# Moving the DRAM weight sums out of the half-size group, and two norm multiplications half a unit later, in a one-core hybrid decoder layer

## The chip, the cores and the metric

The kernel runs on one core of a Trainium2 chip. The metric is the device time of one execution in microseconds (us); lower is better. The core's engines are named as in the profile: PE (TensorE, matmuls), PEld (its weight loads), DVE (VectorE), ACT (ScalarE), POOL (GpSimd) and SP (SyncE). SP and POOL do no arithmetic here that matters; they issue DMA transfers, each from its own queue, in program order. Every engine takes its instructions in the order of its own list, so an instruction that waits holds up all that stand behind it on that engine.

## What is computed

One layer of a decoder for 512 positions and width 1024, in float32: a norm, one wide projection, two token mixers side by side (a block-sparse attention A and an mLSTM B), their gated sum, an output projection, and a SwiGLU feed-forward part, then a last norm. Cut to what matters here:

```python
u = rms_norm(x); z = u @ w_in            # q, k, v | mLSTM q, k, v, gates | branch gates ga, gb
hb = mlstm_chunkwise(q, k, v, i, f)      # (4 heads x 128)
hb = hb * rsqrt(mean(hb * hb) + eps)     # the heads' own norm
yb = sigmoid(ob) * hb * mlstm_norm_g
merged = sigmoid(ga) * (ya @ w_proj_a) + sigmoid(gb) * (yb @ w_proj_b)
h = x + merged @ w_out
u = rms_norm(h); g, up = split(u @ w_gate_up)
h = h + (silu(g) * up) @ w_down
return rms_norm(h)
```

## The kernel before, in words

**Products in three parts.** Each float32 matrix is split into a high and a low part (`split_hl`: ACT rounds the high part, DVE subtracts to get the low part), and a product is three matmuls: high by high, low by high, high by low. A weight block arrives by DMA as `raw` (128 x 1024, 512 KB), is split into `wh` (ACT) and `wl` (DVE), and is then multiplied on PE.

**Seven products instead of eight.** The projection for `gb` and the two large matrices of the feed-forward part are computed as 2 x 2 block products by a scheme with seven block products, named W11, S1, S2, W12, S3, S4, W22. The S blocks of the weights are sums of W blocks. Many of these sums are not made on an engine: a generator, `sum_steps`, makes them in DRAM, each by a copy (SP's queue, L854) into a scratch tensor `ws` and then an adding transfer onto it (POOL's queue, L857). There are 48 such steps: 8 for `gb` (called gs), then copies and additions for five pairs of feed-forward weights (gc0, ds0, gc1, ds1 and so on, S1 and S3 of each). A gc transfer is 1 MB, a ds transfer 512 KB. `make_sums(n)` issues steps until n have been issued; each step waits for the matmul that was last recorded in `st["mm"]` at that point, and this paces the transfers by PE's progress.

**Units.** The work up to the feed-forward part is a list of 66 units, each with one raw weight block: 0 to 13 are q, k, v and two output gates of the mixers, 14 to 17 `vb`, 18 to 25 `qkb`, 26 and 27 `ob`, 28 to 35 `ga`, 36 to 49 `gs` (the half-size group: seven products of two units each, 12 matmuls in a unit and not 24), 50 to 57 `p` (the two branch projections of one column block), 58 to 65 `wo`. `fill` runs the next unit: it first splits the weights of units ahead (two ahead, three within the gs group: before unit 44 runs, unit 47 is split), then calls `make_sums`, then runs the unit's matmuls. Attention and mLSTM steps are woven between the units. `PE` meets all of them in one fixed order.

**Loads.** Raw blocks lie in nine buffers; a load is issued on SP's queue when the split of an older block has freed its buffer. Copies for the sums stand in the same queue between the loads.

**The heads' norm.** After the last mLSTM head, `ml_norm` (L1864 on) takes the root on DVE and ACT, stores the four rows to DRAM (`nd`, POOL, L1873) and reads them back spread over all partitions (`nb`, POOL, L1876, one transfer for heads 0 and 1 and one for heads 2 and 3). `ml_e(h)` then multiplies: L1890 by `nb`, L1891 by the norm weight and the sigmoid of `ob`, both on DVE, then a split into `yb` (ACT and DVE). Heads 2 and 3 also have to be issued after the evacuation of S3 (L663). The order at the end of the mixers is: one unit, `ml_norm`, four gs units (40 to 43), `ml_e(0)`, `ml_e(1)`, two gs units (44, 45), `ml_e(2)`, `ml_e(3)`, the remaining gs units (46 to 49), then the p units, which need `yb` in the second half of each.

**Feed-forward part.** Items gc0, gc1, ds0, gc2, ds1, gc3, ds2, gc4, ds3, then a remainder. A gc item is seven products of 5.44 us, a ds item seven of 2.72 us. In `gc_run` one more sum step is issued with some of the products. Its loads have due times of their own (`GLD`, `plan`), so that a block's load does not move when a sum step moves.

A planner orders the instructions of each engine by priority (in the manner of a list, with its own model of when an operand is ready), so the order on an engine follows the program's order closely but not exactly.

Of the kernel before, what the change touches and what calls it, by code (L numbers as in the profile page):

```python
# [76 lines left out]
G0 = UNITS.index(("gs", 0))  # L77
# [22 lines left out]
def hybrid_layer_kernel(ctx: ExitStack, tc, xT, wall, wgb, wgc, wgu, wds, wdl, g3v, vecs, wgates, consts, rope, out):  # L100
    nc = tc.nc
    V, A, T = nc.vector, nc.scalar, nc.tensor
# [11 lines left out]
    def nm(p="t"):  # L114
        cnt[0] += 1
        return f"{p}{cnt[0]}"

    def slot(dt=F32, name="a"):
        return act.tile([P, S], dt, name=nm(name), tag="A")
# [11 lines left out]
    def mmb():  # L131
        return psum.tile([P, S], F32, name=nm("mm"), tag="mm", bufs=3)
# [120 lines left out]
    for k in range(KT):  # L253
        for j in (0, 2) if k == 0 else (0,):
            c = slice(j * P, (j + 2) * P if k == 0 else S)
# [27 lines left out]
    uh, ul = [], []  # L283
# [23 lines left out]
    for k in range(KT):  # L307
        if k < 4:
            t = blk2(F32R, "u", raw=k < 2)
            h, l = t[:, 0, :], t[:, 1, :]  # L310
        else:
            h, l = slot(F32R, "uh"), slot(F32R, "ul")
        wh, wl = w0h[k // 4][:, k % 4], w0l[k // 4][:, k % 4]
        halves = [(0, 1), (2, 3)] if k == 0 else [range(4)]
        c = slice(0, P * len(halves[0]))
# [12 lines left out]
        for js in halves:  # L328
            if js[0]:
                c = slice(2 * P, S)  # L330
# [67 lines left out]
    def fill(n=1, mid=None):  # L398

        for _ in range(n):  # L400
            u = pos[0]
            if u >= len(UNITS):
                if mid:
                    mid()
                return
            kind, i = UNITS[u]
            ahead = min(u + LOOK + 1, max(u, G0 + 2 * len(GW))) if kind == "gs" else u + LOOK
            while wstate["split"] <= min(ahead, NGEN - 1):
                split_unit()
            pos[0] += 1  # L410
            v = u if u < G0 else max(u + G0, 2 * u - 2 * len(GW)) // 2
            make_sums(5 * (min(v, G0 + 4) - 19) // 4 + 3 * max(v - G0 - 10, 0) // 4)
            g = run[kind](i, *whl.pop(u))
            next(g, None)
            if mid:
                mid()
            for _ in g:
                pass
# [10 lines left out]
    st = {"made": 0}  # L429
# [49 lines left out]
    def run_v(kind):  # L479
        def products(ps, t, units):  # L480
            c = slice(t * P, (t + 1) * P)
            for j, (wh, wl) in units:
                for e in range(2):
                    k = 2 * j + e
                    h, l = wh[:, S * e : S * e + S], wl[:, S * e : S * e + S]
                    T.matmul(ps, uh[k][:, c], h, start=k == 0, stop=False)
                    T.matmul(ps, uh[k][:, c], l, start=False, stop=False)
                    T.matmul(ps, ul[k][:, c], h, start=False, stop=k == KT - 1)

        def evacuate(ps, t):  # L490
            c = slice(t * P, (t + 1) * P)
            for j in range(2):
                d = st[kind, j]
                o = ps[:, 256 * j : 256 * j + 256]
                if kind == "va":

                    o = o.rearrange("p (h d) -> p h d", h=4)
                    h, l = d[:, :, t * P : t * P + 64], d[:, :, t * P + 64 : (t + 1) * P]
                else:
                    o = o.rearrange("p (h d) -> p h d", h=2)  # L500
                    h, l = d[:, 0:4:2, c], d[:, 1:4:2, c]
                act_(h, o, AF.Copy, scale=rt[:, t : t + 1])
                V.scalar_tensor_tensor(l, o, rt[:, t : t + 1], f(h), op0=ALU.mult, op1=ALU.subtract)

        def fn(i, wh, wl):
            if i == 0:
                st[kind] = []
                st[kind, "ps"] = [mmb(), mmb()]
                for j in range(2):
                    d = st[kind, j] = slot4(F32R, kind)  # L510
                    if kind == "vb":
                        vml[2 * j], vml[2 * j + 1] = (d[:, 0, :], d[:, 1, :]), (d[:, 2, :], d[:, 3, :])
                    for e in range(4 if kind == "va" else 0):
                        vat[4 * j + e] = d[:, e, :]
            st[kind].append((i, (wh, wl)))
            for t in range(2):
                products(st[kind, "ps"][t], t, st[kind][-1:])
            yield
            if i == 3:
                for t in range(2):  # L520
                    evacuate(st[kind, "ps"][t], t)
                for t in range(2, 4):
                    ps = accb() if kind == "va" else mmb()
                    products(ps, t, st[kind])
                    evacuate(ps, t)
        return fn
# [370 lines left out]
    def make_sums(n):  # L897

        while st["made"] < n:
            st["made"] += 1  # L900
            i = next(making, None)
            if i is not None:
                tc.add_manual_dep(raw_ins(i), raw_ins(st["mm"]).name, after, reason="paced")
# [96 lines left out]
    def gc_run(c):  # L1000

        key = ("gc", c)
        g = sw.pop(key)
        two = range(2)

        def product(ps, w, o, first=False):
            make_sums(st["made"] + (w in (("S4", "W22"), ("W11", "S2", "S3", "W22"))[c > 0]))
            for j, (wh, wl) in enumerate(g[w]):
                for t in two:
                    at(key, w, 2720 * j + 1360 * t)  # L1010
                    q = slice(t * P, (t + 1) * P)
                    for e in range(2):
                        k = 2 * j + e
                        bh, bl = (b[:, q] for b in bop(o, k))
                        d = slice(e * S, (e + 1) * S)
                        st["mm"] = T.matmul(ps[t], bh, wh[:, d], start=first and k == 0, stop=False, skip_group_check=not first)  # L1016
                        T.matmul(ps[t], bh, wl[:, d], start=False, stop=False, skip_group_check=not first)  # L1017
                        T.matmul(ps[t], bl, wh[:, d], start=False, stop=k == 3, skip_group_check=not first)  # L1018

        def done(w, t):  # L1020
            at(key, w, 4080 + 1360 * t)

        def copies(ps, w, name):
            r = []
            for t in two:
                done(w, t)
                r.append(slot(name=name))
                act_(r[t], ps[t], AF.Copy)
            return r

        X = [mmb() for _ in two]
        product(X, "W11", 0, first=True)
        a = copies(X, "W11", "ga")
        Z = [sb() for _ in two]
        product(Z, "S1", 1, first=True)
        x3 = copies(Z, "S1", "gx")
        product(X, "S2", 4)
        b = copies(X, "S2", "gb")
        yield
        if c == 0:  # L1040
            second_norm(key)
        rg = st["rg"]
        Y = [accb() for _ in two]
        product(Y, "W12", 2, first=True)
        for t in two:
            done("W12", t)
            V.tensor_tensor(a[t], Y[t], a[t], op=ALU.subtract)
        yield
        product(X, "S3", 5)
        for t in two:  # L1050
            done("S3", t)
            V.tensor_tensor(x3[t], X[t], x3[t], op=ALU.add)
            act_(x3[t], x3[t], AF.Silu, scale=rg[:, t + 2 : t + 3])
        yield
        ht = slot4(name="ht").rearrange("p j (b h e x) -> p (j b) h e x", h=2, e=32, x=2)

        def turn(t, u, s):
            V.tensor_tensor(u, u, s, op=ALU.mult)
            V.transpose(ht[:, :, t // 2, :, t % 2], u.rearrange("p (b e) -> p b e", e=32))

        product(Z, "S4", 3)
        for t in two:
            done("S4", t)
            V.tensor_tensor(b[t], Z[t], b[t], op=ALU.add)
            at(key, "W22", 1360 * t)
            turn(t + 2, b[t], x3[t])
        product(X, "W22", 6)
        for t in two:
            done("W22", t)
            s = slot(name="gs")  # L1070
            act_(s, X[t], AF.Silu, scale=rg[:, t : t + 1])
            turn(t, a[t], s)
        at(key, "W22", 5440 + 3000)
        d = hid_t[c] = dram.tile([P, 4, S], F32, name=nm("ad"))
        for i in range(4):
            nc.sync.dma_start(
                d[:, i].rearrange("(g o) x -> o g x", o=32), ht[32 * i : 32 * i + 32].rearrange("p (g b) h e x -> p g (b h e x)", g=4)
            )
# [835 lines left out]
    while n < len(steps) or qa or qb:  # L1914
        if qa and (len(qa) >= LA or n >= len(steps)):
            kind, h, b, r = qa.pop(0)
            qb.append((kind, h, b, moba_b(h, b, r) if kind == "a" else r, n))
        if n < len(steps):
            kind, h, b = steps[n]
# [9 lines left out]
        def mid():  # L1929
            for g in todo.pop(n, ()):  # L1930
                add(g)
            advance(2 if n < 13 else 3)
            second()
# [9 lines left out]
        while qb and (qb[0][4] <= n - LC):  # L1943
            kind, h, b, r, _ = qb.pop(0)
# [14 lines left out]
        drain()  # L1959
    fill(1)  # L1960
    ml_norm()
    fill(4)
    ml_e(0)
    ml_e(1)
    fill(2)
    ml_e(2)
    ml_e(3)
    while pos[0] < len(UNITS) and UNITS[pos[0]][0] != "p":
# [102 lines left out]
```

## Time and profile before

| what | value |
|---|---|
| time, median of 3 runs | 716.77 us (715.41 to 717.86) |
| the profiled execution's own time | 716.61 us |
| its span, first to last instruction | 714.8 us |
| PE busy | 701.3 us, 98% of the span |
| DVE busy | 609.6 us, 85% |
| ACT busy | 460.9 us, 64% |
| moved by DMA | 170.79 MB, mean 239 GB/s |
| mean granted PE clock | 0.993 |

How to read it: PE's busy time is close to the span, so time is lost only where PE waits or where its clock is lowered, and at the two ends. The views used below are the page, tables of windows (busy time of each engine in a stretch, then the granted clock, then the busy share of the 16 DMA engines, then GB/s), lists of waits (total us, times, longest), and timelines of single engines (start, duration, engine, line, operation, tiles, count, and in brackets the idle time before it with what ended it). Times are us from the start of the span.

### The profile page before, as it was taken

Reading aid. Unit: us, or ns where it says so; the run is one execution under the profiler, and the core shown is the slowest. Engines: PE = TensorE matmul, PEld = TensorE weight load, DVE = VectorE, ACT = ScalarE, POOL = GpSimd, SP = SyncE. Lnnn points to the kernel's source line nnn. Section 1 sums busy time; section 2 is a strip of 40 time slices with the busy share of each in tenths; the row PEclk is TensorE's granted clock in tenths of the full one; section 3 lists DMA queues with packets and bytes.
Section 4 is the critical chain, followed back from the end, with each engine's and each line's share of the span. In section 5 each row is a group of like instructions: output and inputs, shape, how many; then the busy total and the mean of one; then the engine's idle time right before and its main releaser. Section 6 shows DMA issues by size and latency. Waiting matters only on the chain.

```text
span 714.8 us, 9624 instructions
## 1 busy us (share of the span) xinstructions
PE 701.3 (98%) x3248; PEld 582.6 (82%) x3248; DVE 609.6 (85%) x1009; ACT 460.9 (64%) x788; POOL 83.2 (12%) x118
## 2 busy tenths in 40 slices
PE   9999999999999999799999999999999999999995
PEld 6888888887888888688888888888888888888884
DVE  6888977898996866978699888898899899797996
ACT  6634888769784786567354756566765666575665
POOL 0013010000130001020010110012003004003000
PEclk9999999999999999899999999999999999999999
DMA  9769684479899899699987578889899959969703
GB/s 326 290 198 242 202 228 147 162 229 297 207 296 332 240 251 277 253 283 335 297 217 185 198 218 240 315 229 300 295 268 279 264 155 221 314 157 271 221 1 117
DMA packets 54881, 170.79 MB, mean 239 GB/s; under 512 B 6472, under 2 KB 10960, under 8 KB 49328
## 3 DMA queue, kind: packets, MB, share of 16 engines
q1 hardware_dynamic: 42544, 126.76, 51.2%
q0 software_dynamic: 12000, 42.87, 28.3%
q10 hardware_dynamic: 288, 0.56, 0.2%
q8 instruction: 25, 0.41, 0.2%
q14 instruction: 24, 0.20, 0.1%
HBM read 145.99 MB, written 64.01 MB: 294 GB/s over the span
## 4 chain that ended last, share of the span: by engine, by line
PE 77%; DVE 14%; ACT 4%; issue 2%; DMA 1%; DVEq 0%; ACTq 0%
PE mm L231 7%; PE mm L227 7%; PE mm L230 7%; PE mm L1017 5%; PE mm L1018 5%; PE mm L1016 5%; PE s L1017 3%; PE s L1018 3%; PE s L1016 3%; PE mm L1262 2%; PE mm L1264 2%; PE mm L1261 2%; PE mm L334 2%; PE acc L334 2%; DMA ws<-in_wgc_dram 1%
## 5 line engine op out<-in xcount | busy, mean ns | idle before, releaser
L163 ACT ACTIVATE w<-raw 128x1024 fp32r<-128x1024 f32 (+2 forms) x107 | 108.1, 1023 | 48.7 <-PE mm L1017 18.7
L991 DVE TENSOR_TENSOR w<-raw,w 128x1024 fp32r<-128x1024 f32 x70 | 84.4, 1220 | 19.8 <-ACT w L163 19.5
L176 DVE TENSOR_TENSOR wl<-raw,wh 128x1024 fp32r<-128x1024 f32 x62 | 75.2, 1221 | 16.2 <-ACT wh L163 16.1
L163 ACT ACTIVATE wh<-raw 128x1024 fp32r<-128x1024 f32 x62 | 65.1, 1054 | 31.1 <-PE mm L230 27.7
L1016 PE MATMUL mm<-w,bq 128*128 128x512 f32 x160 | 62.2, 389 | 0.0
L1017 PE MATMUL mm<-w,bq 128*128 128x512 f32 x160 | 62.2, 389 | 0.0
L1018 PE MATMUL mm<-w,bq 128*128 128x512 f32 x160 | 62.2, 389 | 0.0
L227 PE MATMUL mm<-u,wh 128*128 128x512 f32 x96 | 37.8, 394 | 0.0
L231 PE MATMUL mm<-u,wh 128*128 128x512 f32 x96 | 37.5, 391 | 0.0
L230 PE MATMUL mm<-u,wl 128*128 128x512 f32 x96 | 37.5, 390 | 0.0
L231 PE MATMUL mm<-ul,wh 128*128 128x512 f32 x96 | 37.4, 389 | 0.0
L227 PE MATMUL mm<-uh,wh 128*128 128x512 f32 x96 | 37.4, 389 | 0.0
L230 PE MATMUL mm<-uh,wl 128*128 128x512 f32 x96 | 37.3, 389 | 0.0
L1016 PEld LDWEIGHTS mm<-w,bq 128*128 128x128 f32 x160 | 30.0, 188 | 6.3
L1017 PEld LDWEIGHTS mm<-w,bq 128*128 128x128 f32 x160 | 30.0, 188 | 6.2
L1018 PEld LDWEIGHTS mm<-w,bq 128*128 128x128 f32 x160 | 30.0, 188 | 6.2
L1172 DVE TENSOR_TENSOR w<-raw,w 128x1024 fp32r<-128x1024 f32 x25 | 30.3, 1218 | 1.3 <-ACT w L163 1.2
L1261 PE MATMUL mm<-w,ac 128*128 128x512 f32 x80 | 31.2, 389 | 0.0
L1262 PE MATMUL mm<-w,ac 128*128 128x512 f32 x80 | 31.2, 389 | 0.0
L1016 PE MATMUL s<-w,bq 128*128 128x512 f32 x80 | 31.1, 389 | 0.0
L1017 PE MATMUL s<-w,bq 128*128 128x512 f32 x80 | 31.1, 389 | 0.0
L1018 PE MATMUL s<-w,bq 128*128 128x512 f32 x80 | 31.1, 389 | 0.0
(495 smaller groups left out, 2019.3 us busy)
## 6 DMA issues: line engine op xcount, KB each, us to landing
raw<-in_wall_dram SPq DMA_DIRECT2D x48, 512.0 KB, 6.0
raw<-ws SPq DMA_DIRECT2D x38, 512.0 KB, 6.9
raw<-in_wgc_dram SPq DMA_DIRECT2D x30, 512.0 KB, 7.5
ws<-in_wgc_dram SPq DMA_DIRECT2D x10, 1024.0 KB, 8.1
ws<-in_wgc_dram POOLq DMA_DIRECT2D x10, 1024.0 KB, 11.0
raw<-in_wds_dram SPq DMA_DIRECT2D x15, 512.0 KB, 7.6
ws<-in_wds_dram SPq DMA_DIRECT2D x10, 512.0 KB, 6.3
ws<-in_wds_dram POOLq DMA_DIRECT2D x10, 512.0 KB, 7.7
```

Of the source, the lines that this page charges most:

```text
L163: return A.activation(out_, in_, func, **kw)
L176: last["v"] = V.tensor_tensor(l, src, f(h), op=ALU.subtract)
L227: st["mm"] = T.matmul(ps, wh[:, c], rh[j], start=start and j == 0, stop=False)
L230: T.matmul(ps, wl[:, c], rh[j], start=False, stop=False)
L231: T.matmul(ps, wh[:, c], rl[j], start=False, stop=stop and j == n - 1)
L991: V.tensor_tensor(l, t, f(h), op=ALU.subtract)
L1016: st["mm"] = T.matmul(ps[t], bh, wh[:, d], start=first and k == 0, stop=False, skip_group_check=not first)
L1017: T.matmul(ps[t], bh, wl[:, d], start=False, stop=False, skip_group_check=not first)
L1018: T.matmul(ps[t], bl, wh[:, d], start=False, stop=k == 3, skip_group_check=not first)
L1172: V.tensor_tensor(w[k][1], g[k], f(w[k][0]), op=ALU.subtract)
L1261: T.matmul(ps, bh, wh[:, d], start=first and k == 0, stop=False, skip_group_check=not first)
L1262: T.matmul(ps, bl, wh[:, d], start=False, stop=False, skip_group_check=not first)
```

## The change

```diff
@@ fill
             v = u if u < G0 else max(u + G0, 2 * u - 2 * len(GW)) // 2
-            make_sums(5 * (min(v, G0 + 4) - 19) // 4 + 3 * max(v - G0 - 10, 0) // 4)
+            make_sums(5 * (min(v, G0) - 17) // 4 + 3 * max(v - G0 - 10, 0) // 4)
@@ run_v, products
-                    T.matmul(ps, uh[k][:, c], h, start=k == 0, stop=False)
+                    i = T.matmul(ps, uh[k][:, c], h, start=k == 0, stop=False)
+                    if kind == "vb":
+                        st["mm"] = i
@@ gc_run, product
-            make_sums(st["made"] + (w in (("S4", "W22"), ("W11", "S2", "S3", "W22"))[c > 0]))
+            make_sums(st["made"] + (w in (("S4", "W22"), ("W11", "S1", "S2", "S3", "W22"), ("W11", "S2", "S3", "W22"))[min(c, 2)]))
@@ the end of the mixers
     fill(1)
     ml_norm()
-    fill(4)
+    fill(5)
     ml_e(0)
     ml_e(1)
-    fill(2)
+    fill(1)
     ml_e(2)
     ml_e(3)
```

`G0` is 36, the first gs unit. The formula in `fill`, worked out for every unit, gives:

| units | sum steps issued before | sum steps issued after |
|---|---|---|
| 18 to 35 | 1 to 20 (the first at unit 20) | 1 to 22 (the first at unit 18) |
| 36 to 49 (gs) | 21 to 26, at units 36, 38, 40, 42 (two), 44 | 23, at unit 36 |
| 50 to 65 (p, wo) | 27 to 35, from unit 55 on | 24 to 32, from unit 55 on |
| gc0, gc1, gc2, gc3, gc4 | 2, 4, 4, 3, 0 | 2, 5, 4, 4, 1 |

Up to unit 36 every step comes two units sooner. Step 24 is the copy for gc2's S1, 25 the addition for ds1's S3, 26 the copy for gc2's S3. The three steps that the gs group no longer issues are caught up in the feed-forward part, in gc1, gc3 and gc4. The change in `run_v` adds no instruction: it records the `vb` units' matmuls, so that the step now issued at unit 18 waits for unit 17. The last part puts gs unit 44, with the split of unit 47 that goes ahead of it, in front of `ml_e(0)` and `ml_e(1)`; `ml_e(2)` and `ml_e(3)` keep their place after unit 45. No arithmetic is added or removed.

## The prediction

> **What bounds the kernel now.** I read the page's busy times first, then the waits of PE, then PE, DVE and POOL in order of time around the longest wait.
>
> ```profile
> PE 701.3 (98%) x3248; PEld 582.6 (82%) x3248; DVE 609.6 (85%) x1009; ACT 460.9 (64%) x788; POOL 83.2 (12%) x118
> PE s L639 <- DVE wl L176: 3.5, 1, 3.5
> PE s L250 <- DVE mask L238: 1.0, 1, 1.0
> ```
>
> PE is busy for 98% of the span, so there is little to win anywhere but in PE's waits. Only one is longer than 1 us: a matmul of the gs group that waits for the low part of a weight block.
>
> ```profile
> 283.50 0.39 PE L638 MATMUL s<-wh,uh 128*128 128x512 f32 x1
> ...
> 286.22 0.39 PE L638 MATMUL s<-wh,uh 128*128 128x512 f32 x1
> 290.15 0.79 PE L639 MATMUL s<-wl,uh 128*128 128x512 f32 x1 [3.54 <-DVE wl L176]
> ...
> 301.06 0.39 PE L227 MATMUL mm<-ya,wh 128*128 128x512 f32 x1
> 292.00:294.00 2.00, 2.00 (x6) 1.59 (x5) 2.00 (x4) 0.00 (x0) 0.00 (x0) 0.50 0.51 170
> ```
>
> A gs unit of 12 matmuls takes 286.22 - 283.50 = 2.72 us, 0.227 for each matmul. At 286.22 unit 47 (second half of S4) begins, and units 47, 48 and 49 should be through at 286.22 + 3 x 2.72 = 294.38, when the first p unit could begin. It begins at 301.06. **The place costs 6.68 us**, not 3.54: after the wait the granted clock is 0.50 (last row, third number from its end), and some 12 matmuls run at half speed.
>
> ```profile
> 279.48 1.30 DVE L666 STREAM_TRANSPOSE gt<-gW 128x512 f32<-128x512 f32 x2
> 286.34 1.29 DVE L1890 SCALAR_TENSOR_TENSOR nsb<-nb,nsb 128x512 f32<-128x512 f32 x2 [5.57 <-DMA nb<-nd]
> ...
> 288.88 1.22 DVE L176 TENSOR_TENSOR wl<-raw,wh 128x1024 fp32r<-128x1024 f32 x1
> 290.01 1.29 DVE L176 TENSOR_TENSOR yb<-nsb,yb 128x512 fp32r<-128x512 f32 x2
> 291.21 1.22 DVE L176 TENSOR_TENSOR wl<-raw,wh 128x1024 fp32r<-128x1024 f32 x1
> 292.35 1.41 DVE L663 SCALAR_TENSOR_TENSOR gS<-mm,nrt,gS 128x512 f32<-128x512 f32 x2
> ...
> 294.89 1.25 DVE L1890 SCALAR_TENSOR_TENSOR nsb<-nb,nsb 128x512 f32<-128x512 f32 x2
> ...
> 297.38 1.22 DVE L176 TENSOR_TENSOR wl<-raw,wh 128x1024 fp32r<-128x1024 f32 x1
> ```
>
> DVE stood idle for 5.57 us ahead of the first norm multiplication, waiting for `nb`. The split of unit 47 (288.88) is queued behind the four multiplications of heads 0 and 1, though its operands had long been there. So PE waits for a DMA that it does not need yet. From 286.34 on DVE has no gap: splits 47 and 48, two `yb` splits, S3's evacuation, four more multiplications, split 49.
>
> ```profile
> 272.31 0.60 POOL L1873 DMA_DIRECT2D nd<-fl  x1 [4.33 <-DVE fl L357]
> 272.90 0.86 POOL L857 DMA_DIRECT2D ws<-in_wds_dram  x1
> 277.73 1.13 POOL L1876 DMA_DIRECT2D nb<-nd  x2 [3.97 <-DMA nd<-fl]
> DMA to landing us min/median/max: 8.6/10.0/11.4
> 277.80 10.37 DMA ws<-in_wgc_dram
> ```
>
> Why `nb` is late: the 8 KB store `nd` is issued at 272.31, an addition for the sums (step 25) goes right behind it, `nb` can be issued only at 277.73, and its first transfer lands 8.6 us later. The last row is from the chain that ended last: it names the copy of step 26, which landed at 288.17, as what released a multiplication. That instruction reads no `ws` and DVE had no gap there, so I go by the wait on `nb`. Both transfers lie in the same stretch, and the change touches both.
>
> **The change part by part.**
>
> *No sums in the gs group.* Steps 22 to 26 leave it (3.5 MB, of them step 25 on POOL between `nd` and `nb`, and copies 24 and 26 on SP). What `nb` then costs isn't in the trace, so it is bounded.
>
> ```profile
> 414.01 0.52 POOL L1136 DMA_DIRECT2D row<-vec  x1 [7.70 <-DVE vec L357]
> 416.83 0.74 POOL L1137 DMA_DIRECT2D rg<-row  x1 [2.31 <-DMA row<-vec]
> h1d<-ht POOLq DMA_DIRECT2D x4, 256.0 KB, 4.8
> R<-scr POOLq DMA_DIRECT2D x4, 640.0 KB, 9.3
> ```
>
> The nearest store-then-load on POOL took 416.83 - 414.01 = 2.82 us, against 5.42 here, so `nb` is issued at about 272.31 + 2.82 = 275.1 (at worst 277.7). For its landing the rows on the same queue go from 4.8 us (256 KB) to 9.3 (640 KB, spread over the partitions like `nb`); I take the middle, 7.05, and get T = 282.2 for the time when `nb` is there. Bounds: 275.1 + 4.8 = 279.9 and, nothing gained, 286.34.
>
> *Norm multiplications one gs unit later.* Split 47 now stands ahead of `ml_e(0)`. DVE is free at 279.48 + 1.30 = 280.78; split 47 takes 290.01 - 288.88 = 1.13 and ends at 281.9, well ahead of unit 47's second matmul at 286.45. So the old wait goes. What is late next is **split 49**, still behind all eight multiplications. It ended 297.38 + 1.22 - 286.34 = 12.26 us after the first of them, 11.13 without split 47. Unit 49 would begin at 286.22 + 2 x 2.72 = 291.66, and its second matmul needs split 49 at 291.89. With T = 282.2 the split ends at 282.2 + 11.13 = 293.3: PE waits r = 1.4 us. By the bounds of T: r = 281.9 + 11.13 - 291.89 = 1.15 if `nb` is there by 281.9, and 5.6 if it still lands at 286.34. Split 48 (291.21 + 1.14 - 286.34 - 1.13 = 4.9 after T) ends at 287.1, ahead of its need at 289.2.
>
> Whether a wait of 1.4 us also costs clock lies between two rows.
>
> ```profile
> 173.64 0.55 PE L1735 MATMUL s<-con,P 128*128 128x128 f32 x3 [0.61 <-ACT P L168]
> 170.00:180.00 10.00, 9.39 (x50) 7.68 (x49) 9.94 (x28) 8.97 (x20) 0.00 (x0) 1.00 0.75 254
> ```
>
> After 0.61 us of idle PE the clock stayed at 1.00; after 3.54 it was 0.50, which cost 6.68 - 3.54 = 3.1 us, less 0.4 for a short second wait. I take no drop, since 1.4 is nearer to 0.61; the other end, 2.7 us more, is kept. The Trainium skill (TensorE: Matmul & The Clock Gate, "Part 1: The HAM clock gate") puts the drop to half rate after an idle window of about 3.4 us, free-running: by that rule a wait of 1.4 us costs no clock, and by the upper bound 711.3 below would become 714.0.
>
> *First sums two units sooner.* Copies and additions of steps 1 to 20 move ahead, past splits, loads and the reads of `R` in the SP and POOL queues. On POOL the tight one is the read of `R` for head 3.
>
> ```profile
> 196.47 0.58 POOL L1767 DMA_DIRECT2D R<-scr  x1 [9.53 <-PE s L1800]
> 204.66 0.35 DVE L1779 SCALAR_TENSOR_TENSOR R<-con,cS,R 128x128 f32<-128x128 f32 x1 [0.26 <-DMA R<-scr]
> 208.22 1.22 DVE L176 TENSOR_TENSOR wl<-raw,wh 128x1024 fp32r<-128x1024 f32 x1
> 219.05 0.40 PE L227 MATMUL mm<-u,wh 128*128 128x512 f32 x1
> ws<-in_wgc_dram POOLq DMA_DIRECT2D x10, 1024.0 KB, 11.0
> 263.52 3.22 SPq L207 DMA_DIRECT2D raw<-in_wgb_dram  x2
> ```
>
> DVE waits for `R` already now, 0.26 us. After the change an addition of 1 MB (11.0 us to landing) goes out shortly ahead of it, so DVE may idle up to 11 us. Cover: the split at 208.22 is for unit 31, whose matmuls begin at 219.05, 9.6 us after the split's end. I cost it at 0, with 11.0 - 9.6 = 1.4 at most; nothing can be gained, as PE has no wait there. SP's loads are far ahead (last row: units 48 and 49 were loaded from 263.5 on, 25 us ahead of their matmuls), so copies among them cost nothing. Recording `vb`'s matmuls adds no instruction.
>
> *Three sums later.* The p and wo units issue nine steps as before, 7 MB as before. The feed-forward part gets 1 MB more in gc1, 1 MB more in gc3 and 0.5 in gc4. I cost that at 0 because loads there are early.
>
> ```profile
> 426.00:464.00 38.00, 38.00 (x169) 31.50 (x168) 33.11 (x39) 22.25 (x30) 1.58 (x2) 1.00 0.88 277
> 483.00:521.00 38.00, 38.00 (x170) 31.46 (x169) 33.96 (x39) 24.87 (x33) 5.12 (x6) 1.00 0.97 288
> 480.01 7.61 SPq L912 DMA_DIRECT2D raw<-in_wgc_dram  x2
> raw<-in_wgc_dram SPq DMA_DIRECT2D x30, 512.0 KB, 7.5
> 514.10 1.07 ACT L163 ACTIVATE w<-raw 128x1024 fp32r<-128x1024 f32 x1
> q0 software_dynamic: 12000, 42.87, 28.3%
> ```
>
> In gc2 (483 to 521) the DMA engines are at 0.97 and PE is still busy for 38.00 of 38.00. The second load of W22 is issued by 480.01 + 7.61 = 487.6 and split at 514.10, 26.5 us later, of which the landing takes some 7.5.
>
> **The sum.** 716.61 (the profiled execution: span 714.8 and 1.8 around it) - 6.68 + 1.4 = **711.3 us**. The median of the runs shown, 716.77, is 0.16 above that execution, within the runs' own scatter (715.41 to 717.86), so I leave it out.
>
> **The rivals.**
>
> *Nothing left.* The planner puts split 49 ahead of heads 2 and 3, or `nb` is early and PE's order gives way: 716.61 - 6.68 = 709.9. For it: DVE idles until `nb` lands, so there is room; against it: in the order before, split 49 stood behind all eight. Chance 0.14.
>
> *The multiplications stay ahead of split 47.* The planner may keep its order; then only the earlier `nb` counts: split 49 ends at 282.2 + 12.26 = 294.5, r = 2.6, 712.5. Against it: the program's order is changed there, and it was followed before. Chance 0.09.
>
> *`nb` isn't sooner.*
>
> ```profile
> 280.00:290.00 10.00, 6.61 (x30) 5.14 (x28) 4.43 (x7) 1.67 (x3) 0.00 (x0) 0.94 0.98 375
> ```
>
> If loads of p units fill the freed DMA time, T stays 286.34 and r = 5.6, split into 2.1 ahead of unit 48 and 3.5 ahead of unit 49: 715.5, or 718.2 if the second one drops the clock again. For it: the DMA engines were at 0.98 in that stretch (last number but one); against it: the loads are paced by DVE's splits, one 512 KB block in 2.72 us. Chance 0.15, mostly the lower value.
>
> *The sums that were moved cost PE time later (slower).* The additions' queue took 28.3% of 714.8 us for 42.87 MB, 4.7 us of all engines per MB. In 426 to 464 (gc1) 12% of 38 us are free, 4.6 us, and 4.7 are added; in gc2 next to nothing is free. If loads then come late, gc1 and gc3 cost up to 4.7 us each: 711.3 + 9.4 = 720.7. It decides once a load lands 26.5 - 7.5 = 19 us later than now. The Trainium skill (DMA: Bandwidth & Descriptors, "Issuing engines are not separate DMA queues") speaks for it: transfers from any engine share the same 16 DMA engines, so moving steps in a queue saves none of their time. Against it stands gc2's full PE at 0.97. With a planner's order that is worse elsewhere, chance 0.12.
>
> **How the numbers follow.** The forecast has 0.50, and with the first two rivals **faster by over 0.3%** (below 714.6, about what a measurement can tell from no change) has 0.73; within 0.3% has the third rival's 0.15; slower has 0.12. The range goes from 709.4 (nothing left, less half a us of scatter) to 716.5, which takes in the third rival without the clock's drop and leaves out some 0.18.
>
> **What would show it.** Split 47 ahead of L1890 on DVE, no wait of PE at unit 47, POOL with nothing between `nd` and `nb`, `nb` issued near 275 and there by about 282, a short wait ahead of unit 49, and a clock of 1.00 through the group. From the first p unit to the end the distance should stay as before. It is wrong if PE waits in 388 to 654, or if `nb` still lands after 285.

## The result, and the profile after

| what | before | after |
|---|---|---|
| time, median | 715.66 us (715.41 to 717.86, 6 runs) | 711.17 us (710.59 to 711.74, 6 runs) |
| the profiled execution's own time | 716.61 us | 711.12 us |
| its span | 714.8 us | 709.3 us |
| mean granted PE clock | 0.993 | 0.997 |

The ratio of the times over all runs is 0.9931, with a 95% interval from 0.9917 to 0.9945 (the two medians alone give 0.9937): the kernel became faster by 0.7%. The page's busy times hardly show it, since PE's share stays at 98%:

```profile
PE 698.6 (98%) x3248; PEld 580.7 (82%) x3248; DVE 609.1 (86%) x1009; ACT 459.9 (65%) x788; POOL 83.1 (12%) x118
```

To find where the time went, mark the same matmuls in both traces: the first of unit 35, of the first p unit and of gc0. The timeline of PE before has two of them here (the third, 301.06, is in the prediction):

```profile
246.88 0.40 PE L227 MATMUL mm<-u,wh 128*128 128x512 f32 x1
...
388.39 0.39 PE L1016 MATMUL mm<-w,bq 128*128 128x512 f32 x1
```

and the timeline of PE after has, beside these three, the one matmul in the stretch that waits:

```profile
246.97 0.40 PE L227 MATMUL mm<-u,wh 128*128 128x512 f32 x1
...
293.06 0.50 PE L641 MATMUL mm<-wl,u 128*128 128x512 f32 x1 [0.69 <-DVE wl L176]
...
295.46 0.39 PE L227 MATMUL mm<-ya,wh 128*128 128x512 f32 x1
...
382.79 0.39 PE L1018 MATMUL mm<-w,bq 128*128 128x512 f32 x1
```

| stretch | before | after |
|---|---|---|
| start to unit 35 | 246.88 | 246.97 |
| unit 35 to the first p unit | 54.18 | 48.49 |
| first p unit to gc0 | 87.33 | 87.33 |
| gc0 to the end of the span | 326.41 | 326.51 |

All of the gain, 5.69 us, lies between unit 35 and the first p unit; elsewhere nothing differs by more than 0.1 us. The middle two distances are used for every run below. Next the cause, on POOL's timeline after:

```profile
272.41 0.61 POOL L1875 DMA_DIRECT2D nd<-fl  x1 [19.18 <-DVE fl L357]
275.22 1.11 POOL L1878 DMA_DIRECT2D nb<-nd  x2 [2.19 <-DMA nd<-fl]
```

Nothing stands between `nd` and `nb`, and they are 2.81 us apart instead of 5.42. The list of DMA issues in 262 to 290 (KB each, median us from issue to landing) had, before,

```profile
raw<-in_wall_dram SPq DMA_DIRECT2D x4, 512.0 KB, 11.6
...
nb<-nd POOLq DMA_DIRECT2D x2, 512.0 KB, 10.0
nd<-fl POOLq DMA_DIRECT2D x1, 8.0 KB, 5.1
```

and has after

```profile
raw<-in_wall_dram SPq DMA_DIRECT2D x6, 512.0 KB, 3.6
...
nb<-nd POOLq DMA_DIRECT2D x2, 512.0 KB, 5.7
nd<-fl POOLq DMA_DIRECT2D x1, 8.0 KB, 2.5
```

These three land in 31% to 57% of the time they took, the plain weight loads too: the stretch as a whole is less loaded. DVE's timeline after shows what became of its stall:

```profile
280.79 1.18 DVE L176 TENSOR_TENSOR wl<-raw,wh 128x1024 fp32r<-128x1024 f32 x1
281.90 1.28 DVE L1892 SCALAR_TENSOR_TENSOR nsb<-nb,nsb 128x512 f32<-128x512 f32 x2
...
284.42 1.22 DVE L176 TENSOR_TENSOR wl<-raw,wh 128x1024 fp32r<-128x1024 f32 x1
...
291.79 1.22 DVE L176 TENSOR_TENSOR wl<-raw,wh 128x1024 fp32r<-128x1024 f32 x1
292.93 1.29 DVE L176 TENSOR_TENSOR yb<-nsb,yb 128x512 fp32r<-128x512 f32 x2
```

The first row is split 47, then the first norm multiplication follows with no bracket, so without idle time: `nb` was there. Splits 48 and 49 follow at 284.42 and 291.79; split 49 is the one that is late, by 0.69 us. The waits of PE after (total us, times, longest) no longer hold anything over 1 us:

```profile
PE s L250 <- DVE mask L238: 1.0, 1, 1.0
PE s L1737 <- ACT P L168: 0.9, 2, 0.6
PE mm L641 <- DVE wl L176: 0.7, 1, 0.7
```

The tables of windows after (length, PE busy, PEld, DVE, ACT, POOL, clock, DMA share, GB/s) show the clock at 1.00 around the old wait, and PE without any gap in the feed-forward part, which got 2.5 MB more of sums:

```profile
286.00:295.00 9.00, 8.31 (x37) 6.55 (x36) 9.00 (x14) 3.52 (x5) 0.00 (x0) 1.00 0.48 166
...
388.00:654.00 266.00, 266.00 (x1188) 220.48 (x1187) 234.50 (x275) 168.54 (x224) 41.58 (x50) 1.00 0.89 259
```

### The profile page after: what moved, and what is told of

Its sections match the earlier page's. It is cut to its first block, busy times and chain, and to the rows that moved or that the text cites. A ratio compares the mean times of both kernels' runs of the same rounds, so it can differ in the third digit from the quotient of the medians.

```text
span 709.3 us, 9628 instructions
## 1 busy us (share of the span) xinstructions
PE 698.6 (98%) x3248; PEld 580.7 (82%) x3248; DVE 609.1 (86%) x1009; ACT 459.9 (65%) x788; POOL 83.1 (12%) x118
## 4 chain that ended last, share of the span: by engine, by line
PE 80%; DVE 14%; ACT 4%; issue 2%; ACTq 0%; DVEq 0%
PE mm L231 8%; PE mm L227 8%; PE mm L230 7%; PE mm L1018 5%; PE mm L1019 5%; PE mm L1020 5%; PE s L1018 3%; PE s L1019 3%; PE s L1020 3%; PE mm L1263 2%; PE mm L1264 2%; PE mm L1266 2%; PE mm L334 2%; DVE wl L176 2%; PE acc L334 2%
```

## The experiments

Each run was timed beside the kernel before on the same chip. That kernel's median was 716.63 us for the first eight and 717.03 for the last three, so the ratios, not the times, are to be compared. The edits are against the kernel before where the text says so, else against the changed one.

### The parts by themselves

**Only the order of the norm multiplications**, on the kernel before:

```diff
-    fill(4)
+    fill(5)
     ml_e(0)
     ml_e(1)
-    fill(2)
+    fill(1)
```

> The kernel before with the last part of the change alone (one more gs unit ahead of heads 0 and 1), sums as before. My theory: the addition still stands between the store nd and the read nb, so nb lands near 286.3 and the chain of DVE work up to split 49 ends 11.1 us later, at 297.4; PE no longer waits at unit 47, but about 2.0 us ahead of unit 48 and 3.5 us ahead of unit 49. Time 715 to 718, within 1.5 us of the kernel before on either side, the upper end if the clock drops. Rival (the order alone cures it): 711 to 712, one wait of about 1 us.

Measured: 714.85 us, ratio 0.9978 [0.9969, 0.9987]; unit 35 to p 51.89. PE's waits in that run:

```profile
PE mm L639 <- DVE wl L176: 2.0, 1, 2.0
PE mm L638 <- DVE gS L663: 1.9, 1, 1.9
```

The 3.5 us at unit 47 are gone, and two shorter ones stand in their place, at units 48 and 49. The first of them is not for split 48, as I had it, but for L663, the evacuation of S3 that frees the output buffer into which unit 48 writes; the split and the evacuation stand in one row on DVE behind `nb`. By the timeline they are 1.96 and 1.85 us, and in the profiled execution the clock did not fall after either. This execution need not be typical: its mean clock, 0.998, is the highest of the run's eleven, and eight of the others had 0.994 or 0.995, like the profiles in which the clock is seen to fall (0.993 to 0.995). Yet their times (714.01 to 716.29 us) lie on both sides of the profiled one's 715.11; why is open. The order alone is worth a third of the change, because `nb` is as late as before.

**Only the sums moved**, with the old order of the multiplications:

```diff
-    fill(5)
+    fill(4)
     ml_e(0)
     ml_e(1)
-    fill(1)
+    fill(2)
```

> The changed kernel with the old order of the norm multiplications (four gs units ahead of heads 0 and 1). My theory: nb is issued near 275.2 and landed by 281, about when DVE comes free, so split 47 behind the four multiplications ends near 284.5 and is in time, and split 49 ends 12.26 us after 280.9, at 293.1, as in the changed kernel. Time 711.2, within 0.5 us of the changed kernel; the order is worth nothing once nb is early. Rival (both parts are needed): a wait of PE at unit 47 and 713 to 716.

Measured: 711.62 us, ratio 0.9929 [0.9917, 0.9942]; unit 35 to p 48.53. That is the whole gain: the order is worth nothing once `nb` is early. PE's only wait in the group is the one that the changed kernel has:

```profile
PE mm L641 <- DVE wl L176: 0.7, 1, 0.7
```

### Why the norm's transfer was late

Two things went from the stretch: the addition that stood between `nd` and `nb` in POOL's queue, and two copies of 1 MB on SP's queue, beside them. **First the queue position**, on the kernel before: the addition of step 25 is issued behind `nb` (its place in the order of steps is changed with the copy of step 26).

```diff
@@ sum_steps, on the kernel before
-            prev = None
+            prev, late = None, []
...
-                    if prev:
+                    if key == ("gc", 2, "S1"):
+                        late.append(prev)
+                    elif prev:
+                        while late:
+                            yield added(*late.pop())
```

> The kernel before, but with steps 25 and 26 exchanged, so that POOL's addition for ds1 is issued behind nb and no longer between nd and nb; the copies on SP stay in the gs group, one of them sooner. If the queue is what held nb (the addition ahead of it in POOL's queue): nb is issued near 275.2 and lands in 5.4 to 8.6 us, at 280.6 to 283.8; waits of 1 to 4 us in all, 711.3 to 713.5. Rival (the busy DMA engines are what held it): nb lands at 285 or later and the time stays at 715 to 716.5.

Measured: 716.5 us, ratio 0.9999 [0.9991, 1.0008]; unit 35 to p 53.79. POOL's timeline:

```profile
272.31 0.60 POOL L1877 DMA_DIRECT2D nd<-fl  x1 [4.32 <-DVE fl L357]
277.85 1.11 POOL L1880 DMA_DIRECT2D nb<-nd  x2 [4.94 <-DMA nd<-fl]
278.95 0.86 POOL L857 DMA_DIRECT2D ws<-in_wds_dram  x1
```

POOL has nothing between the two any more and sits idle for 4.94 us: it is the 8 KB store itself that takes so long. The theory that the addition held `nb` back in the queue fell here. The edit has a side effect, though: both copies now go out in one piece. SP's timeline before had

```profile
272.36 0.50 SPq L854 DMA_DIRECT2D ws<-in_wgc_dram  x1
...
277.80 0.50 SPq L854 DMA_DIRECT2D ws<-in_wgc_dram  x1
```

and has in this run

```profile
272.38 1.14 SPq L854 DMA_DIRECT2D ws<-in_wgc_dram  x2
```

So beside the store the addition (512 KB) was exchanged for a second copy (1 MB), not merely taken away.

**Then the addition's load**, on the kernel before: the same edit as above, and step 26 of that order put off to the p units, so that the addition is gone from the group and both copies stay (again both right behind the store).

```diff
@@ fill, beside the edit of sum_steps above
-            make_sums(5 * (min(v, G0 + 4) - 19) // 4 + 3 * max(v - G0 - 10, 0) // 4)
+            make_sums(min(5 * (min(v, G0 + 4) - 19) // 4, 25) + (1 if u >= 55 else 0) + 3 * max(v - G0 - 10, 0) // 4)
```

> The kernel before, but in the gs group POOL's addition (step 25) is put off to the p units, while both 1 MB copies stay (both issued near 272.4). If the copies' load held nb: nd still takes 4 to 5 us and nb 7 to 8, landed at 284 to 286, 714.5 to 716.5. Rival (the addition's traffic was the larger part): nb by 282 and 711.5 to 713.

Measured: 716.58 us, ratio 1.0004 [0.9995, 1.0012]; unit 35 to p 54.00. POOL:

```profile
272.48 0.60 POOL L1877 DMA_DIRECT2D nd<-fl  x1 [4.33 <-DVE fl L357]
277.65 1.11 POOL L1880 DMA_DIRECT2D nb<-nd  x2 [4.57 <-DMA nd<-fl]
```

and SP at the same time:

```profile
272.54 1.14 SPq L854 DMA_DIRECT2D ws<-in_wgc_dram  x2
```

Without the addition nothing is gained: the store goes out at 272.48, and right behind it 2 MB of copies. The time lies just above the range that was expected if the copies' load is the cause (714.5 to 716.5).

**Last the copies' load**, on the kernel before: copies 24 and 26 put off to the p units, the addition kept between `nd` and `nb`.

```diff
@@ fill, on the kernel before
-            make_sums(5 * (min(v, G0 + 4) - 19) // 4 + 3 * max(v - G0 - 10, 0) // 4)
+            make_sums(min(5 * (min(v, G0 + 4) - 19) // 4, 24) + (2 if u >= 55 else 0) + 3 * max(v - G0 - 10, 0) // 4)
@@ sum_steps
+                    if key == ("gc", 2, "S1"):
+                        yield added(*prev)
+                        prev = None
```

> The kernel before, but in the gs group the two 1 MB copies on SP (steps 24 and 26) are put off to the p units, while POOL's addition (step 25) stays between nd and nb. The exchange of steps 25 and 26 did not help, so POOL's queue is not what held nb. If the copies' load on the DMA engines held it: nd takes 3 to 4 us, nb 5.5 to 7, landed by 281 to 284, one wait of PE of 1 to 3 us, 711.5 to 714. Rival (the addition's own traffic suffices): nb at 285 or later and 715 to 716.5.

Measured: 715.1 us, ratio 0.9981 [0.9969, 0.9992]; unit 35 to p 51.60. POOL:

```profile
272.02 0.60 POOL L1876 DMA_DIRECT2D nd<-fl  x1 [4.33 <-DVE fl L357]
272.60 0.86 POOL L857 DMA_DIRECT2D ws<-in_wds_dram  x1
275.23 1.12 POOL L1879 DMA_DIRECT2D nb<-nd  x2 [1.77 <-DMA nd<-fl]
```

| kernel | between `nd` and `nb` | 2 MB of copies | `nd` to `nb` issued, us | `nb` to landing (median), us | PE's wait |
|---|---|---|---|---|---|
| before | addition | there, 5.4 us apart | 5.42 | 10.0 | 3.54 |
| addition behind `nb` | nothing | there, both behind `nd` | 5.54 | 9.0 | 3.09 |
| addition off | nothing | there, both behind `nd` | 5.17 | 9.7 | 3.38 |
| copies off | addition | gone | 3.21 | 7.7 | 1.95 |
| only the sums moved | nothing | gone | 2.92 | 6.3 | 0.68 |
| after | nothing | gone | 2.81 | 5.7 | 0.69 |

(The landings are those of the lists of DMA issues in 262 to 290.) The clean comparison for the copies is the first row with the fourth: they are worth 2.2 of the gap and 2.3 of the landing. In the gap it is the first copy alone, as the second goes out at 277.80, behind `nb` (277.73). What the addition is worth while the copies stay in their old places no run shows, because the second and third rows have a copy more beside the store. With the copies gone, the additions are worth at most 0.3 to 0.4 of the gap and 1.4 to 2.0 of the landing (fourth row against the last two). These are two additions, since the last two rows also issue that of step 23 sooner: at unit 36 (252.45 after) and not 5 us ahead of the store (267.19 before).

So what was removed is load on the DMA engines: in the gap mostly the copies', in the landing the copies' and the additions' in nearly equal parts. For the gap the place in POOL's queue is not what counts: before, too, POOL had done with the addition and sat idle for 3.97 us until the store had landed. In the landing the additions' place and their load are not told apart. The Trainium skill (DMA: Bandwidth & Descriptors, "Issuing engines are not separate DMA queues") says that transfers issued from different engines share the same 16 DMA engines; the runs agree: copies on SP's queue delayed a store on POOL's by 2.2 us (5.42 - 3.21).

The run without the copies brought less than its shorter wait would say. `nb` was there by 281.97 and PE had one wait of 1.95 us, as the theory said, but the median of 715.1 us lies outside its range (711.5 to 714) and in the rival's. In the profiled execution (713.9 us; the twelve go from 713.57 to 716.75) the stretch became 2.58 of the 5.69 us shorter. Its windows (columns as above):

```profile
292.00:294.00 2.00, 0.34 (x2) 0.00 (x0) 2.00 (x3) 1.47 (x2) 0.00 (x0) 1.00 0.81 272
294.00:298.00 4.00, 3.71 (x10) 2.96 (x11) 4.00 (x7) 2.27 (x4) 0.00 (x0) 0.62 0.91 277
```

After the wait of 1.95 us the clock fell, to 0.62 on average over 294 to 298, and the place cost 51.60 - 47.50 = 4.1 us, more than twice the wait (47.50 is the distance without any wait, from the next run).

### The wait that is left

**Heads 2 and 3 later as well**: the changed kernel, with `ml_e(2)` and `ml_e(3)` two units later, behind split 49.

```diff
     ml_e(0)
     ml_e(1)
-    fill(1)
+    fill(3)
     ml_e(2)
     ml_e(3)
```

> The changed kernel with heads 2 and 3 multiplied two gs units later (behind unit 47), so that splits 49 and 50 stand ahead of their four multiplications. My theory: the wait of about 1 us ahead of unit 49 is the DVE chain alone, so it goes: 710.2 to 710.5, no wait of PE in the group. Rival (DVE's work is only shifted, and another piece is late next, split 51 or yb of heads 2 and 3 in the first p unit): 711.0 to 712.0 with a wait in the first two p units.

Measured: 711.55 us, ratio 0.9933 [0.9920, 0.9945]. Unit 35 to p is 47.50, 0.99 less than after: the wait at unit 49 is gone. But p to gc0 is 88.22, 0.89 more. Two of PE's waits are new:

```profile
PE mm L227 <- ACT g L163: 0.6, 1, 0.6
...
PE mm L1018 <- ACT gs L168: 0.5, 1, 0.5
```

The multiplications are work that DVE has to do in any case; put off, they make later rows late. The rival was right.

**Work taken off DVE for good**: the changed kernel, with the low parts of `yb` for heads 0 and 1 subtracted on POOL, which has nothing to do there.

```diff
@@ ml_e
-        yb[h] = split_hl(t, dst=pair4("yb", h))
+        if h < 2:
+            hi, lo = pair4("yb", h)
+            act_(hi, t, AF.Copy)
+            nc.gpsimd.tensor_tensor(lo, t, f(hi), op=ALU.subtract)
+            yb[h] = hi, lo
+        else:
+            yb[h] = split_hl(t, dst=pair4("yb", h))
```

> The changed kernel, but the low parts of yb for heads 0 and 1 are subtracted on POOL, and their rounded parts come from ACT; so two subtractions of about 1.2 us each leave the row of DVE work ahead of split 49. My theory (the wait ahead of unit 49 is DVE work that does not fit ahead of the split): split 49 ends about 1.1 to 2.4 us sooner, no wait of PE at unit 49, p begins 47.5 us after unit 35 instead of 48.49, and since the work has left DVE for good nothing comes back later: 710.2 to 710.7. Rival 1 (as with heads 2 and 3 put off, DVE is only late elsewhere): the wait comes back in the p units, 711.2 to 711.7. Rival 2 (POOL's subtraction or its issue is late for the first use of yb): a wait of PE at the p units on yb, over 712.

Measured: 710.35 us, ratio 0.9913 [0.9899, 0.9926]. POOL takes 3.46 us for the two subtractions, for which DVE took 1.28, and is done long before p:

```profile
285.11 3.46 POOL L1897 TENSOR_TENSOR yb<-nsb,yb 128x512 fp32r<-128x512 f32 x2 [8.16 <-ACT yb L163]
```

PE's list of waits shows none in the gs group:

```profile
PE s L250 <- DVE mask L238: 1.0, 1, 1.0
PE s L1737 <- ACT P L168: 0.9, 2, 0.6
PE acc L1185 <- DVE w L963: 0.6, 1, 0.6
```

Unit 35 to p is 47.53 and p to gc0 87.39, so 0.96 us are gone from the trace and nothing comes back. The intervals of this run and of the changed kernel overlap; that it is faster than the changed kernel rests on the trace more than on the times.

### The sums that were moved

**The feed-forward part as before**: the three moved steps are caught up in the p and wo units.

```diff
@@ fill
-            make_sums(5 * (min(v, G0) - 17) // 4 + 3 * max(v - G0 - 10, 0) // 4)
+            make_sums(5 * (min(v, G0) - 17) // 4 + (3 * max(v - G0 - 10, 0) // 4 if u < 55 else max(u - 53, 0)))
@@ gc_run, product
-            make_sums(st["made"] + (w in (("S4", "W22"), ("W11", "S1", "S2", "S3", "W22"), ("W11", "S2", "S3", "W22"))[min(c, 2)]))
+            make_sums(st["made"] + (w in (("S4", "W22"), ("W11", "S2", "S3", "W22"))[c > 0]))
```

> The changed kernel with the three steps that moved into the feed-forward part caught up in the p and wo units, so that from gc0 on the sums are those of the kernel before. My theory: the moved steps cost PE nothing in the feed-forward part, so nothing is won: 710.8 to 711.7. Rival (they cost DMA time there that PE feels): faster than the changed kernel by over 0.7 us.

Measured: 710.7 us, ratio 0.9923 [0.9911, 0.9935]; the two distances are 48.49 and 87.33, as after. So the sums in the feed-forward part cost nothing that can be measured there, nor do they in the p units.

**The first sums not sooner**: the formula starts two units later again, and the two steps that are then missing are caught up at the first p unit.

```diff
@@ fill
-            make_sums(5 * (min(v, G0) - 17) // 4 + 3 * max(v - G0 - 10, 0) // 4)
+            make_sums(5 * (min(v, G0) - 19) // 4 + (2 if u >= 50 else 0) + 3 * max(v - G0 - 10, 0) // 4)
```

> The changed kernel with the first sums at unit 20 again: the gs group issues step 21 alone, two more are issued at unit 50, the rest as in the changed kernel. My theory: coming two units sooner is worth nothing by itself, it only makes room; 711.2 to 711.8, within 0.6 us of the changed kernel. Rival (sooner sums matter, or the two steps caught up at the first p unit collide with its loads): 713 or more, with a wait of PE after 295.

Measured: 716.1 us, ratio 0.9994 [0.9984, 1.0004]: the whole gain is lost. Yet the gs group is as good as after (unit 35 to p 48.47). The loss is behind it, p to gc0 91.22, with two new waits:

```profile
PE mm L227 <- DVE ga L698: 2.0, 1, 2.0
PE mm L227 <- ACT pb L163: 1.3, 1, 1.3
```

SP issued the copy at 295.59, and POOL's timeline goes on:

```profile
295.86 0.82 POOL L859 DMA_DIRECT2D ws<-in_wds_dram  x1 [19.09 <-PE mm L641]
310.04 2.22 POOL L678 DMA_DIRECT2D gb<-gd  x4 [13.36 <-DMA gd<-gt]
```

Here the branch gate is stored (`gd`) and read back (`gb`) for the p units, another round trip through DRAM, and the two sums fell right ahead of it. That could be the cause, or it could be that two steps less ahead of the gs group are a loss wherever they are caught up. **The same with the catch-up five units later** tells these apart:

```diff
-            make_sums(5 * (min(v, G0) - 19) // 4 + (2 if u >= 50 else 0) + 3 * max(v - G0 - 10, 0) // 4)
+            make_sums(5 * (min(v, G0) - 19) // 4 + (2 if u >= 55 else 0) + 3 * max(v - G0 - 10, 0) // 4)
```

> The run in which the first sums weren't sooner, but the two steps are caught up five units later, at the sixth p unit instead of the first. My theory (the 3.9 us lost in that run came of the place of the catch-up, where an addition and a copy met the gd stores and gb loads; sums two units sooner are worth nothing by themselves): from the first p unit to gc0 about 87.3 instead of 91.22, 711.0 to 711.8. Rival (two steps less before the gs group are the loss, wherever they are caught up): again 90 or more, 715 to 716.5. Second rival (the new place collides with something else): a wait of PE between these, 712.5 to 715.

Measured: 711.66 us, ratio 0.9934 [0.9920, 0.9947]; the distances are 48.52 and 87.33. POOL's timeline:

```profile
305.88 2.14 POOL L678 DMA_DIRECT2D gb<-gd  x4 [29.31 <-DMA gd<-gt]
```

`gb` is issued at 305.88 and not at 310.04 (after: 305.58). So it was the place of the catch-up, and sums two units sooner are worth nothing by themselves.

### A version of both

**The feed-forward sums as before and the low parts of `yb` on POOL**, the two edits shown above together.

> The run with the feed-forward sums as before, and the low parts of yb for heads 0 and 1 on POOL besides: a version that may beat both kernels. My theory: both parts add up, 709.5 to 710.3. Rival (the p units have no room for three more sums when DVE's or POOL's order changes): 711 or more.

Measured: 710.21 us, ratio 0.9908 [0.9894, 0.9923], the lowest of all. From the run with `yb` on POOL alone it can't be told apart; the distances are 47.52 and 87.39.

## Why the prediction was right

**Forecast and time.** 711.3 was predicted for the profiled execution, which took 711.12; the runs' median is 711.17.

- *The place costs 6.68 us.* Right. The three runs without a wait in the group have 47.50 to 47.53 from unit 35 to p, the kernel before 54.18: 6.65 to 6.68 more.
- *`nd` to `nb` in 2.82 us, `nb` issued at about 275.1.* Right: 2.81, at 275.22. But the prediction named the addition behind `nd` and the copies side by side and didn't say which of them holds `nb` back. The runs say that it is load on the DMA engines, in this gap the copies' first of all (2.2 us of the 2.6). The number came out because the change takes out both, and that it agrees to 0.01 us is luck: the row it was taken from has the DMA engines 0.49 busy (414 to 417), the new place 0.75 (272 to 276), and with only the sums moved the same pair took 2.92. It was also said that steps 22 to 26, 3.5 MB, leave the group; by the table of units step 23 stays, at unit 36. It is gone from the stretch that counts, so the sum doesn't change.
- *`nb` lands in 7.05 us, T = 282.2.* Mis-sized: the first landing took 5.4 us (the middle one 5.7), T = 280.6. It cost nothing, as DVE is busy until 281.90 anyway. The step that counts is then the lower bound that the prediction gave for an `nb` there by 281.9.
- *Split 47 ahead of the multiplications takes the old wait away.* The order is as predicted and it does take this wait away, but an early `nb` does so too: with the old order and the moved sums the time is the same. By itself the order brought 0.2%, in the way that the rival "`nb` isn't sooner" described: 715.5 worked out, 714.85 measured. That rival's wait at unit 48 was put to the wrong instruction, the split and not the evacuation, and its sum of 5.6 us came out as 51.89 - 47.50 = 4.4.
- *Split 49 is late by r = 1.4 us.* Right in place, smaller in size: 48.49 - 47.50 = 0.99, of which 0.69 is the wait that the profile names. The row of DVE work up to the end of split 49 took 292.93 - 281.90 = 11.03, where 11.13 was forecast. By the bound for an early `nb` r would have been 1.15. The size of r and the landing are the only terms of the sum that were off, and the forecast would have been 711.1 by 1.15.
- *No fall of the clock.* Right: 1.00 in 286 to 295. As the wait came out at 0.69 us, what 1.4 us would have done was not put to the test; that the bound of 2.7 us was kept is borne out by the run without the copies, where 1.95 us of wait cost 4.1.
- *First sums sooner, three sums later: 0.* Right. The slower rival, 720.7 through late loads in the feed-forward part, did not come: PE was busy for 266.00 of 266.00 us there. In the stretch that answers to the one quoted for gc1, 5.6 us sooner, the DMA share rose from 0.88 to 0.93 at full PE:

```profile
420.40:458.40 38.00, 38.00 (x169) 31.38 (x168) 33.94 (x41) 23.65 (x32) 2.54 (x3) 1.00 0.93 286
```

The mechanism that the rival needs does exist, but elsewhere: the run with two steps caught up at the first p unit lost 3.9 us by it, where a round trip through DRAM had little slack. The loads of the feed-forward part had.

## What to carry to other kernels

A small round trip through DRAM (a store of 8 KB, then a broadcast read) on which an engine waits is held up by bulk transfers of any queue, so move the bulk out of its stretch; putting it behind the small transfers in their own queue won nothing here (that run also sent a copy sooner). Put what you move where nothing makes such a round trip: the same two sums cost 3.9 us at one unit and nothing five units later. And where an engine's row of work is the limit, putting work off moves the wait, while giving it to an idle engine, even one that takes 2.7 times as long (3.46 against 1.28 us), removes it.

## What the runs showed of the hardware that was not expected

**The clock and short waits.** In the run without the copies the granted clock fell after a single wait of 1.95 us (0.62 on average over 294 to 298). In the run with the catch-up at the first p unit it stayed at 1.00 after a wait of just that length:

```profile
324.07 0.50 PE L227 MATMUL mm<-yb,wh 128*128 128x512 f32 x1 [1.95 <-DVE ga L698]
322.00:326.00 4.00, 2.05 (x9) 1.61 (x9) 4.00 (x8) 3.38 (x7) 0.00 (x0) 1.00 1.03 398
```

It stayed at 1.00 through 1.31 us in that run too, and through 1.85 and 1.96 us in the profiled execution of the run with only the order changed. After 3.09, 3.38 and 3.54 us it fell to 0.50 in each of the three profiles, after 0.69 in none. So around 2 us the length of the wait alone doesn't decide, and executions of one kernel can differ (mean clocks of 0.994 to 0.998 in the run with only the order changed). The Trainium skill (TensorE: Matmul & The Clock Gate, "Part 1: The HAM clock gate") speaks of an idle window of about 3.4 us that runs freely. A window whose place varies would fit two like waits that end differently. But 1.95 us is shorter than that figure, and the measurement decides; what sets the fall is open.

**A small store under load.** The same 8 KB store landed in 2.5 us with the stretch's copies and additions gone (the DMA engines 0.56 busy in 262 to 290) and in 5.1 with them there (0.94), though it has less than a hundredth of the bytes of one copy.
